# A lone first tile in the batches of a decoder step, its stages interleaved with the next batch's projections, gathers paced closer

## The chip, the cores and the metric

One of the eight cores of a Trainium2 chip runs the kernel. The metric is the device time of one launch in microseconds (us), as the median over several runs; beside it stands one execution that was profiled, from which all rows below come.

## What is computed

One layer of a decoder for a prompt of 1024 tokens (eight tiles of 128) and a sample of 8 x 8 tokens (tile 8, 64 rows), both with the same weights, in float32 with D = 1024:

```
h   = x @ w_in                                # 1024 -> 3072: gate MLP (u, v), retention (q, k, v, g)
mix = concat(spatial_gate(u, v), retention(q, k, v)) @ w_o
x   = layer_norm(ALPHA * x + mix)             # ln1
x   = layer_norm(ALPHA * x + attention(x @ ca_wq, 256 memory tokens) @ ca_wo)   # ln2
q   = x @ peer_wq                             # 8 heads, two halves of 128 keys each
    top 16 of each half -> 256 candidates -> top 16 -> softmax g
act = gelu(u_tab[eidx] . x)                   # 128 experts of 16384 for every token
x   = layer_norm(ALPHA * x + sum(g * act * v_tab[eidx]))                        # ln3
```

The retention carries a state from tile to tile, so the prompt's tiles run in order. The sample attends to its own cached keys and values, 64 blocks of 256 KB.

## The kernel before

Two Python generators emit the whole program. `main` (`front`, then `dense`) and `gathers` each keep an order clock; the one that is behind emits next (the loop at the end of `body`). The clocks are no times: `W.mm` adds 1.3 for every two weight blocks, `front` adds 0.5 when a chunk is done for a tile, a gather adds COST_U (the first 128) or COST_G. The clock becomes the priority from which a list scheduler makes each engine's in-order queue.

**The front** goes through `plan`, a list of (batch, weight, chunk). A weight chunk is 1024 x 512, eight blocks of 256 KB loaded on SP's queue into a ring of NR = 10 (`Weights.load`, line 141). For each chunk all tiles of the batch multiply it (line 149; float32 takes two passes, so 16 passes of 512 columns for a tile and chunk), accumulate in one of three PSUM banks (`mm` twice, `mx` once), and start a generator of small steps (`post_gate`, `post_ret`, `post_res`, `post_att`, `post_att_s` for the sample, `post_peer`) that `step_all` moves on by one step after each quarter chunk. Each batch goes through w_in (6 chunks), w_o, wq, wo (2 each) and pq (4, the expert selection); batch 0 has the memory's wk and wv as well. SPREAD places the pq chunks of one batch between the w_in chunks of the next. Batches before: (0 1), (2 3 8), (4 5), (6 7).

**Experts by gather**, for the tiles in GT = 0, 8, 5, 6, 7: `jobs` lists 576 U gathers and 576 V gathers, one row for each of 128 tokens, 512 KB each, in the order JORD. Each is an indirect DMA that POOL issues (lines 1133, 1136) into one of NG = 6 buffers. A U row set is multiplied and summed on DVE (the dot, line 1068); V rows are combined on PE (line 1096, in pairs). U gathers of a tile need its selection (pq chunk by chunk), V gathers need all of it. The use of a gather is emitted LAG = 3 gathers after its issue.

**Experts by dense matmul**, for the tiles in DT = 1 to 4: after the last pq chunk of such a tile, `post_peer` builds a table G of the gate weights of all 16384 experts: for four tokens at a time one-hot operands (lines 707 to 714, ACT and DVE), four matmuls into the one `gb` bank (line 718), a copy on ACT into the one buffer `big` (line 722), and after 16 tokens a 1 MB store to DRAM (line 726). The flag `gsl` lets one tile build at a time; `gok` (the plan's entry GOK, batch 2's first w_in chunk) lets the first begin. `dense` then streams the whole U and V tables once, 128 blocks: line 977 (h), gelu and the multiplication by G, line 1022 (accumulate), line 1029 (sum on DVE). It reads G back before its first products, and its buffers for V take the place of the table builder's.

`finish` normalises a tile and stores it (line 900). NAT and NA are the numbers of row tiles and of transposed half tiles that the front may hold; `rot` holds the rotary angles of a tile.

Of the kernel before, what the change touches and what calls it, by code (L numbers as in the profile page):

```python
# [22 lines left out]
ALPHA = 2.0 ** 0.25  # L23
EPS = 1e-5
GAM = [1.0 - 2.0 ** (-5.0 - h) for h in range(4)]
BATCHES = [[0, 1], [2, 3, 8], [4, 5], [6, 7]]
TLS = True
MS = ""
SC = 100
# [25 lines left out]
PQT = 2  # L55
PQ = 2
PS = 2
SPREAD = ((0,2,3,5),(0,1,3,4))
PIN = 1
PO = 0  # L60
PG = 0
PC = 0
PP = 0
NR = 10
NAT = 4
NA = 12
NG = 6
LAG = 3
NFL = 4
ND = 2  # L70
GT = [0,8,5,6,7]
DT = [1,2,3,4]
JORD = ("u0","v0","u8","u5 v8","u6 v5","u7 v6","v7")
FB = 2
COST_G = 1.4
COST_U = 1.9
NEG = -3.0e38


def rows(t):  # L80
    return 64 if t == SMP else 128
# [78 lines left out]
def body(ctx: ExitStack, tc: tile.TileContext, a):  # L160
# [14 lines left out]
    def T(shape, tag, bufs=1, dt=F32):  # L175
        return sb.tile(shape, dt, name=tag, tag=tag, bufs=bufs)
# [42 lines left out]

    seq = []  # L220
    plan = []
    for bi in range(len(BATCHES) + 1):
        pq = [(bi - 1, "pq", c) for c in range(4)] if bi else []
        if bi < len(BATCHES):
            names = ("w_in",) * 6 + (() if bi else ("wk",) * 2 + ("wv",) * 2) + ("w_o",) * 2 + ("wq",) * 2 + ("wo",) * 2
            for j, name in enumerate(names):
                plan.append((bi, name, j if j < 6 else j % 2))
                for c in range(4):
                    if pq and SPREAD[bi == 1][c] == j:
                        plan.append(pq[c])  # L230
        else:
            plan += pq
    for _, name, c in plan:
# [23 lines left out]
    st = {}  # L257
# [141 lines left out]
    def aT_tile(t):  # L399
        if t == SMP:  # L400
            x = T([128, 8, 64], "aT", NA)
            return [x[:, 0:4, :], x[:, 4:8, :]]
        return [T([128, 4, 128], "aT", NA), None]

    def aT_half(t, key, j):
        x = st[key, t]
        if x[j] is None:
            x[j] = T([128, 4, 128], "aT", NA)
        return x[j]
# [22 lines left out]
    def post_res(t, c, p, key, res, which):  # L432
        P = rows(t)
        if c == 0:
            if res is None:
                x = T([128, 1024], "nat", NAT)
                nc.sync.dma_start(x[:P], xslice(t))
# [356 lines left out]
    def front():  # L794
        for i, (bi, name, c) in enumerate(plan):
            batch = BATCHES[bi]
            key = KEY[name]
            if (bi, name, c) == GOK:
                st["gok"] = True
            if bi >= XB and name == "pq":  # L800
                st["mxf"] = True
            if plan[i - 1] == (XB - 1, "pq", 3):
                st["mxf"] = True
            if name == "w_in" and c == 0:
                for t in batch:
                    load_split(t, "xT", a["xsT"] if t == SMP else a["xpT"][t])
                    st["rot", t] = T([128, 2, 128], "rot", 3)
                    nc.scalar.dma_start(st["rot", t], a["rot"][t].rearrange("p (a b) -> p a b", a=2))
                if bi == 0:
                    load_small()  # L810
            if name == "w_in":
                gl = T([128, 2, 256], "gl", 2)
                for j, n in enumerate("gb"):
                    w = WORD[c]
                    if w < 2:
                        nc.sync.dma_start(gl[:, j, :], bc(a["gate_ln_" + n][w * 256:(w + 1) * 256], 256))
                    else:
                        nc.sync.dma_start(gl[:, j, :128], bc(a["ret_gn_" + n][(w - 2) * 128:(w - 1) * 128], 128))
            if name == "pq" and c == 0:
                while fin[0] + NFL < sum(1 for b in BATCHES[:bi + 1] for x in b if x in GT):  # L820
                    yield None
            if name == "pq":
                sub = TQ([128, 4, 128], "sub", 1)
                nc.sync.dma_start(sub, a["subT"][:, 4 * c:4 * c + 4, :])
            if name == "w_o" and c == 0:
                load_ln(1)
            if name == "wo" and c == 0:
                load_ln(2)
            tiles = batch
            if name in ("wk", "wv"):  # L830
                tiles = [0, 1]
                if name == "wk" and c == 0:
                    for t in tiles:
                        load_split(t, "memT", a["memT"][t])
            if name == "wq" and c == 0:
                drain("m")
                load_mem(0)
            ps = {}
            for grp in range(KB // GK):
                for t in tiles:  # L840
                    P = 128 if key == "memT" else rows(t)
                    if grp == 0:
                        if c == 0 and key not in ("xT", "memT"):
                            if name == "w_o":
                                drain(t)
                                add(t, post_cat(t))
                            drain(t)
                        if name == "w_in" and c == 0:
                            st["cat", t] = T([128, 1024], "nat", NAT)
                        ps[t] = MM(bi)  # L850
                    p = ps[t]
                    lt = t == tiles[-1]
                    yield from W.mm(i, grp, p[:P], lhs(key, t), lt)
                    if grp < KB // GK - 1:
                        step_all()
                        continue
                    del ps[t]
                    if c == NCH[name] - 1 and name != "wk":
                        del st[key, t]
                    if name == "w_in":  # L860
                        w = WORD[c]
                        add(t, post_gate(t, w, p, gl) if w < 2 else post_ret(t, w - 2, p, gl))
                    elif name == "w_o":
                        add(t, post_res(t, c, p, "x1", None, 1))
                    elif name == "wq":
                        if c == 1 and t == tiles[0]:
                            for x in tiles:
                                drain(x)
                            load_mem(1)
                        add(t, post_att_s(c, p) if t == SMP else post_att(t, c, p))  # L870
                    elif name == "wo":
                        add(t, post_res(t, c, p, "x2", "x1", 2))
                    elif key == "memT":
                        add("m", post_mem(name, c, t, p))
                    else:
                        add(t, post_peer(t, c, p, sub), True)
                    del p
                    yield 0.5
        while any(not e[2] for e in active):
            step_all()  # L880
            yield 3.0

    fin = [0]
    phase = [0]
    jobs = []
    for grp in JORD:
        parts = [[(x[0], int(x[1]), k) for k in range(rows(int(x[1])))] if x[0] == "u" else
                 [(x[0], int(x[1]), c * 32 + r) for r in range(32) for c in range(rows(int(x[1])) // 32)] for x in grp.split()]
        n = max(len(p) for p in parts)
        for i in range(n):  # L890
            for p in parts:
                jobs += p[i * len(p) // n:(i + 1) * len(p) // n]
# [155 lines left out]
    def gathers():  # L1048
# [70 lines left out]
        for m in range(len(jobs) + LAG):  # L1119
            if m < len(jobs):  # L1120
                kind, t, i = jobs[m]
                P = rows(t)
                need = ("v", t) if kind == "v" else ("u", t, 3 if t == SMP else i // 32)
                while need not in done:
                    yield None
                if kind == "u" and i == 0:
                    x2s[t] = TG([128, 1024], "x2g", 1)
                    for j in range(0, 128, P):
                        nc.sync.dma_start(x2s[t][j:j + P], done["x2", t])
                g = TG([128, 1024], "gbuf", NG)  # L1130
                bufs[m] = g
                if kind == "u":
                    nc.gpsimd.indirect_dma_start(out=g, out_offset=None, in_=a["U"],  # L1133
                                                 in_offset=bass.IndirectOffsetOnAxis(ap=done["ix", t][:, i:i + 1], axis=0))
                else:
                    nc.gpsimd.indirect_dma_start(out=g, out_offset=None, in_=a["V"],  # L1136
                                                 in_offset=bass.IndirectOffsetOnAxis(ap=done["ixT", t][:, i:i + 1], axis=0))
            if m >= LAG:
                use(m - LAG)
            yield COST_U if m < 128 else COST_G  # L1140

    clocks = {"f": 0.0, "g": 0.0}
    gens = {"f": main(), "g": gathers()}
    while gens:
        n = min(gens, key=lambda s: clocks[s])
# [71 lines left out]
```

## Time and profile before

| | us |
|---|---|
| median of 3 runs | 3804.4 (3796.0 to 3805.68) |
| the profiled execution | 3794.4 |
| its span, first to last instruction | 3792.6 |
| PE busy | 3375.7 (89%) |
| DVE busy | 2395.5 (63%) |
| ACT busy | 1160.0 (31%) |
| POOL busy | 1546.8 (41%) |
| DMA | 1039.7 MB, 274 GB/s in the mean |

Busy time is the union of an engine's instructions; PE stands for TensorE's matmuls, DVE for VectorE, ACT for ScalarE, POOL for GpSimd, SP for the engine that issues most plain DMAs. PEclk is the granted TensorE clock as a share of 2.4 GHz; a stretch at 1.2 GHz counts as 0.5. A wait is put down to what came last. The execution has a front (the projections end at 1928) and a dense stage (full from 2040 on); the gathers run beside both.

### The profile page before, as it was taken

How to read it: one execution, taken by the hardware profiler on the slowest of the kernel's cores; microseconds unless marked ns; L12 is line 12 of the kernel's file. 1: busy time of each engine (PE TensorE's matmuls, PEld its weight loads, DVE VectorE, ACT ScalarE, POOL GpSimd, SP SyncE). 2: the span in 40 equal slices, each digit the busy share in tenths (PEclk: the TensorE clock that was granted, in tenths of full speed). 3: DMA queues.
4: the chain of work that ended last, by engine and by line, in shares of the span. 5: the costliest groups of instructions: out<-in, count | busy, mean ns of one | idle time of the engine just before them, and what ended most of it. 6: DMA issues, size and time to landing. Idle time of an engine off the chain costs nothing.

```text
span 3792.6 us, 42587 instructions
## 1 busy us (share of the span) xinstructions
PE 3375.7 (89%) x13881; PEld 2028.0 (53%) x13881; DVE 2395.5 (63%) x6366; ACT 1160.0 (31%) x2256; POOL 1546.8 (41%) x1363
## 2 busy tenths in 40 slices
PE   7988875886999989878866999999999999999993
PEld 3444332343443455445445777777667777767650
DVE  2212677715685537996698887777677777777432
ACT  1121212112453464555454222222223222223211
POOL 0000254614254434554433445454444554444443
PEclk9999886887999999988988999999999999999995
DMA  5544475666888789887866989998888989998976
GB/s 192 198 128 152 136 238 211 217 226 237 284 283 286 263 287 334 292 308 254 312 228 230 328 301 336 336 343 312 315 320 315 334 326 330 319 328 297 326 273 232
DMA packets 407358, 1039.72 MB, mean 274 GB/s; under 512 B 37281, under 2 KB 129633, under 8 KB 403041
## 3 DMA queue, kind: packets, MB, share of 16 engines
q0 software_dynamic: 165888, 604.05, 44.3%
q1 hardware_dynamic: 229392, 420.06, 32.5%
q10 hardware_dynamic: 11856, 12.91, 1.0%
q8 instruction: 109, 1.79, 0.2%
q14 instruction: 113, 0.92, 0.1%
HBM read 985.59 MB, written 51.25 MB: 273 GB/s over the span
## 4 chain that ended last, share of the span: by engine, by line
PE 57%; DVE 14%; DMA 13%; issue 11%; POOL 4%; ACT 2%; POOLq 0%; DVEq 0%; SPq 0%; ACTq 0%
PE mm L149 12%; PE h L977 12%; PE mx L149 7%; PE cb L1096 6%; DMA gbuf<-in_V_dram,ixT 6%; DMA gbuf<-in_U_dram,ix 5%; DVE gbuf L1068 4%; PE oa L1022 4%; PE ob L1022 3%; PE od L1022 3%; PE oc L1022 3%; POOL gbuf L1133 2%; PE gb L718 2%; DVE oi L714 1%; POOL gbuf L1136 1%
## 5 line engine op out<-in xcount | busy, mean ns | idle before, releaser
L1133 POOL DMA_INDIRECT gbuf<-in_U_dram,ix x576 | 684.7, 1189 | 878.8 <-DVE hd L1068 476.1
L1136 POOL DMA_INDIRECT gbuf<-in_V_dram,ixT x576 | 634.4, 1101 | 791.5 <-PE cb L1096 359.6
L1068 DVE CUSTOM_DVE_ANT_0 gbuf<-gbuf,x2g 128x1024 f32<-128x1024 f32 x576 | 711.7, 1247 | 361.2 <-DMA gbuf<-in_U_dram,ix 318.2
L149 PE MATMUL mm<-wr,aT 128*128 128x512 f32 (+1 forms) x1632 | 775.4, 614 | 29.9 <-DMA aT<-in_xpT_dram 14.8
L977 PE MATMUL h<-x,uh 128*128 128x512 f32 x2048 | 657.6, 397 | 22.0 <-ACT ga L981 19.4
L149 PEld LDWEIGHTS mm<-wr,aT 128*128 128x128 f32 (+1 forms) x1632 | 292.6, 190 | 414.0 <-issue 366.0
L977 PEld LDWEIGHTS h<-x,uh 128*128 128x128 f32 x2048 | 383.9, 189 | 163.5 <-issue 58.7
L1096 PE MATMUL cb<-gbuf,Z 128*32 128x512 f32 x2304 | 348.4, 642 | 80.4 <-DMA gbuf<-in_V_dram,ixT 78.5
L149 PE MATMUL mx<-wr,aT 128*128 128x512 f32 (+1 forms) x800 | 391.2, 621 | 25.5 <-ACT ret L333 12.9
L977 PE MATMUL h<-x,ul 128*128 128x512 f32 x1024 | 404.2, 395 | 0.0
L917 ACT ACTIVATE vh<-vr 128x1024 fp32r<-128x1024 f32 x128 | 135.3, 1059 | 502.5 <-PE od L1022 494.0
L149 PEld LDWEIGHTS mx<-wr,aT 128*128 128x128 f32 (+1 forms) x800 | 148.2, 193 | 216.5 <-issue 182.9
L714 DVE TENSOR_SCALAR oi<-cst,kt 128x128 f32<-128x128 f32 x512 | 173.5, 385 | 118.6 <-PE gb L718 117.6
L718 PE MATMUL gb<-oi,oj 128*128 128x128 f32 x1024 | 168.0, 310 | 68.3 <-ACT big L722 34.1
L977 PEld LDWEIGHTS h<-x,ul 128*128 128x128 f32 x1024 | 193.1, 189 | 58.5 <-issue 17.6
L718 PEld LDWEIGHTS gb<-oi,oj 128*128 128x128 f32 x1024 | 149.8, 216 | 130.4 <-ACT big L722 54.2
L917 ACT ACTIVATE ah<-ga 128x512 fp32r<-128x512 f32 x128 | 80.7, 631 | 440.5 <-DVE ga L984 388.1
L917 ACT ACTIVATE uh<-ur 128x1024 fp32r<-128x1024 f32 x128 | 135.5, 1059 | 254.9 <-PE h L977 250.7
L722 ACT ACTIVATE big<-gb 128x512 f32<-128x512 f32 x128 | 133.9, 1046 | 223.0 <-PE gb L718 203.6
L918 DVE TENSOR_TENSOR ul<-ur,uh 128x1024 fp32r<-128x1024 f32 x128 | 157.3, 1229 | 59.2 <-ACT uh L917 59.2
L1096 PEld LDWEIGHTS cb<-gbuf,Z 128*32 128x32 f32 x2304 | 50.9, 110 | 227.3 <-issue 118.0
L707 ACT ACTIVATE oj<-cst,kt 128x128 f32<-128x128 f32 x512 | 159.0, 386 | 29.2 <-PE sm L550 17.6
(237 smaller groups left out, 4994.7 us busy)
## 6 DMA issues: line engine op xcount, KB each, us to landing
vr<-in_V_dram SPq DMA_DIRECT2D x128, 512.0 KB, 6.3
ur<-in_Ud_dram SPq DMA_DIRECT2D x128, 512.0 KB, 6.9
wr<-in_w_in_dram SPq DMA_DIRECT2D x192, 256.0 KB, 4.3
wr<-in_pq_dram SPq DMA_DIRECT2D x128, 256.0 KB, 6.2
gsc<-big SPq DMA_DIRECT2D x32, 1024.0 KB, 5.9
G<-gsc SPq DMA_DIRECT2D x32, 1024.0 KB, 16.5
wr<-in_w_o_dram SPq DMA_DIRECT2D x64, 256.0 KB, 4.5
wr<-in_wq_dram SPq DMA_DIRECT2D x64, 256.0 KB, 5.9
```

What stands on the lines that cost most here:

```text
L149: self.nc.tensor.matmul(p, lhsT=lT(k), rhs=w, start=k == 0, stop=k == KB - 1)
L707: nc.scalar.activation(oj[:, r, :], iota, AF.Abs, bias=kt[:, 3, tk + r:tk + r + 1])
L714: x = nc.vector.tensor_scalar(oi, iota, kt[:, 0, tk + r:tk + r + 1], kt[:, 2, tk + r:tk + r + 1], op0=ALU.is_equal, op1=ALU.mult)
L718: x = nc.tensor.matmul(g4[:, r * 128:(r + 1) * 128], lhsT=oj[:, r, :], rhs=oi, start=True, stop=True)
L917: nc.scalar.activation(hi, raw, AF.Copy)
L918: nc.vector.tensor_tensor(lo, raw, hi.bitcast(F32), op=ALU.subtract)
L977: nc.tensor.matmul(p, lhsT=w[:, k, :], rhs=x[:, k, :], start=k == 0 and j == 0, stop=k == 7 and j == 2)
L1022: nc.tensor.matmul(o[j], lhsT=A[i][ia][:, n * 128:(n + 1) * 128], rhs=Vw[i][iv][:, j * 512:(j + 1) * 512], start=b == 0 and ia + iv == 0, ...
L1068: dot = nc.vector.tensor_tensor_reduce(out=g, in0=g, in1=x2s[t], scale=1.0, scalar=0.0, op0=ALU.mult, op1=ALU.add, accum_out=hd[t][:, i:i ...
L1096: nc.tensor.matmul(comb[t][c1 // 2][32 * (q + n):32 * (q + n) + 32, :], lhsT=Z[:, z1 + c1, 31 - r1:63 - r1], rhs=g1[:, n * 512:(n + 1) * 5 ...
L1133: nc.gpsimd.indirect_dma_start(out=g, out_offset=None, in_=a["U"], in_offset=bass.IndirectOffsetOnAxis(ap=done["ix", t][:, i:i + 1], axis=0))
L1136: nc.gpsimd.indirect_dma_start(out=g, out_offset=None, in_=a["V"], in_offset=bass.IndirectOffsetOnAxis(ap=done["ixT", t][:, i:i + 1], axis=0))
```

## The change

The batches become (0), (1 2 8), (3 4 5), (6 7). A hand-written order, HEAD, follows the first batch's w_in, wk and wv: two chunks of the lone tile's w_o, wq, wo or pq, then one ("+") of the next batch's six w_in chunks, and so on. For the later batches the pq chunks stand after w_in chunks 0, 1, 3 and 4. There is one more row tile, one more transposed half tile and one more `rot` buffer. Gathers advance the order clock by COST_F = 1.1 as long as the front runs, where before it was 1.9 for the first 128 and 1.4 after; in the dense stage 1.4 stays. JORD names the gather order anew, and a tile's V gathers can be named in halves (a, b).

```diff
-BATCHES = [[0, 1], [2, 3, 8], [4, 5], [6, 7]]
+BATCHES = [[0], [1, 2, 8], [3, 4, 5], [6, 7]]
-SPREAD = ((0,2,3,5),(0,1,3,4))
+SPREAD = (0,1,3,4)
+HEAD = "w_o w_o + wq wq + wo wo + pq pq + pq pq + +"
-NAT = 4
-NA = 12
+NAT = 5
+NA = 13
-JORD = ("u0","v0","u8","u5 v8","u6 v5","u7 v6","v7")
+JORD = ("u0","v0","u8","v8","u5","v5a","u6 v5b","u7 v6","v7")
-COST_U = 1.9
+COST_F = 1.1
...
-    for bi in range(len(BATCHES) + 1):
-        pq = [(bi - 1, "pq", c) for c in range(4)] if bi else []
+    plan += [(0, n, c) for n, k in (("w_in", 6), ("wk", 2), ("wv", 2)) for c in range(k)]
+    ahead = 0
+    for n in HEAD.split():
+        if n == "+":
+            plan.append((1, "w_in", ahead))
+            ahead += 1
+        else:
+            plan.append((0, n, sum(x[:2] == (0, n) for x in plan)))
+    for bi in range(1, len(BATCHES) + 1):
+        pq = [(bi - 1, "pq", c) for c in range(4)] if bi > 1 else []
         if bi < len(BATCHES):
-            names = ("w_in",) * 6 + (() if bi else ("wk",) * 2 + ("wv",) * 2) + ("w_o",) * 2 + ("wq",) * 2 + ("wo",) * 2
-            for j, name in enumerate(names):
-                plan.append((bi, name, j if j < 6 else j % 2))
-                for c in range(4):
-                    if pq and SPREAD[bi == 1][c] == j:
-                        plan.append(pq[c])
+            for j in range(ahead if bi == 1 else 0, 6):
+                plan.append((bi, "w_in", j))
+                for c, x in enumerate(pq):
+                    if SPREAD[c] == j:
+                        plan.append(x)
+            plan += [(bi, n, c) for n in ("w_o", "wq", "wo") for c in range(2)]
...
-                    st["rot", t] = T([128, 2, 128], "rot", 3)
+                    st["rot", t] = T([128, 2, 128], "rot", 4)
...
+            h = len(part) // 2
+            parts.append({"a": part[:h], "b": part[h:]}.get(x[2:], part))
...
-            yield COST_U if m < 128 else COST_G
+            yield COST_F if phase[0] == 0 else COST_G
```

## Rows read from the trace of the kernel before

**Rows 1.** the page's 40 slices: TensorE's busy tenths

```profile
PE   7988875886999989878866999999999999999993
```

**Rows 2.** windows by stage: length; PE, PEld, DVE, ACT, POOL; clock, DMA share, GB/s

```profile
15.00:182.00 167.00, 157.60 (x440) 75.77 (x440) 40.18 (x164) 29.91 (x70) 8.65 (x16) 0.99 0.58 188
182.00:314.00 132.00, 112.89 (x361) 59.20 (x361) 27.26 (x44) 29.35 (x57) 15.74 (x12) 0.93 0.42 136
314.00:671.00 357.00, 270.26 (x733) 125.70 (x734) 216.84 (x851) 70.46 (x177) 119.04 (x101) 0.80 0.55 183
671.00:951.00 280.00, 227.20 (x825) 105.53 (x825) 132.21 (x265) 59.67 (x133) 116.48 (x80) 0.87 0.67 233
951.00:1242.00 291.00, 284.96 (x1137) 126.97 (x1135) 194.81 (x927) 122.77 (x306) 124.56 (x125) 0.98 0.82 284
1242.00:1424.00 182.00, 166.78 (x750) 86.94 (x750) 86.90 (x315) 99.47 (x232) 69.77 (x68) 0.97 0.79 276
1424.00:1663.00 239.00, 207.32 (x753) 118.50 (x751) 206.54 (x769) 125.54 (x299) 116.80 (x100) 0.91 0.84 304
1663.00:1847.00 184.00, 150.82 (x627) 87.70 (x628) 136.69 (x406) 91.87 (x217) 90.01 (x81) 0.90 0.82 292
1847.00:1928.00 81.00, 81.00 (x304) 40.91 (x302) 64.69 (x266) 35.74 (x86) 32.34 (x30) 0.99 0.80 279
1928.00:2040.00 112.00, 54.29 (x267) 42.40 (x267) 99.01 (x398) 60.96 (x137) 37.01 (x31) 0.73 0.72 244
2040.00:3700.00 1660.00, 1629.30 (x7548) 1154.45 (x7547) 1166.77 (x1921) 422.33 (x535) 780.95 (x686) 0.99 0.89 316
3700.00:3793.00 93.00, 33.09 (x144) 3.78 (x144) 21.52 (x44) 10.69 (x13) 35.22 (x38) 0.53 0.66 229
```

**Rows 3.** windows, line 149 alone: busy us and count of passes

```profile
314.00:671.00 357.00, 207.54 (x417) 78.15 (x418) 0.80 0.55 183
```

**Rows 4.** timeline at the end: start us, us, engine, line, operation, count [idle before]

```profile
3699.65 0.69 DVE L1029 SCALAR_TENSOR_TENSOR acc<-acc,od 128x512 f32<-128x512 f32 x1 [0.20 <-PE od L1022]
...
3765.71 2.38 ACT L1110 ACTIVATE gbuf<-cb 32x512 f32<-32x512 f32 x4 [1.77 <-PE cb L1096]
...
3787.66 1.47 ACTq L900 DMA_DIRECT2D yp_out_dram<-acc  x2
```

**Rows 5.** waits of PE, 314 to 671: us in total, times, longest

```profile
PE sm L318 <- DVE abf L651: 29.0, 1, 29.0
```

**Rows 6.** waits of PE, 1928 to 2040

```profile
PE gb L718 <- ACT big L722: 21.8, 5, 14.1
```

**Rows 7.** windows, line 722 (copy of four tokens of a table)

```profile
888.00:1173.00 285.00, 33.41 (x32) 0.93 0.78 274
1773.00:2020.00 247.00, 33.56 (x32) 0.88 0.76 263
1970.00:2020.00 50.00, 8.50 (x8) 0.80 0.65 222
```

**Rows 8.** windows, line 1096 (combining; four records for one V gather)

```profile
951.00:1242.00 291.00, 53.82 (x320) 8.55 (x320) 0.98 0.82 284
1242.00:1424.00 182.00, 31.25 (x192) 5.16 (x192) 0.97 0.79 276
...
2040.00:3700.00 1660.00, 201.86 (x1496) 29.60 (x1496) 0.99 0.89 316
```

**Rows 9.** windows, line 718 (table matmuls; 256 records a table)

```profile
951.00:1242.00 291.00, 27.41 (x192) 24.69 (x192) 0.98 0.82 284
1242.00:1424.00 182.00, 27.30 (x184) 24.56 (x184) 0.97 0.79 276
```

**Rows 10.** windows, line 1133 (issue of a U gather)

```profile
671.00:951.00 280.00, 82.78 (x59) 0.87 0.67 233
...
2040.00:3700.00 1660.00, 341.93 (x304) 0.99 0.89 316
```

**Rows 11.** timeline of POOL: the first gather

```profile
423.04 1.14 POOL L1133 DMA_INDIRECT gbuf<-in_U_dram,ix  x1 [4.16 <-DVE cd L641]
```

More of the change, by code (lines that the diff above doesn't have):

```diff
@@ L886, in body @@
     for grp in JORD:
-        parts = [[(x[0], int(x[1]), k) for k in range(rows(int(x[1])))] if x[0] == "u" else
-                 [(x[0], int(x[1]), c * 32 + r) for r in range(32) for c in range(rows(int(x[1])) // 32)] for x in grp.split()]
+        parts = []
+        for x in grp.split():
+            t = int(x[1])
+            part = [(x[0], t, k) for k in range(rows(t))] if x[0] == "u" else [
+                (x[0], t, c * 32 + r) for r in range(32) for c in range(rows(t) // 32)]
+            h = len(part) // 2
+            parts.append({"a": part[:h], "b": part[h:]}.get(x[2:], part))
         n = max(len(p) for p in parts)
```

## The prediction

> **What bounds the kernel now.** I read the page first, then one table by stage, then the places where that table shows a loss. The page's slices show where PE has room: sevens and eights in the first half, nines in the second, a drop in the last slice [rows 1]. The stage table is cut where the plan's chunks begin; 16 passes of line 149 are one tile against one weight chunk (I call that a tile-chunk), so the passes between two times tell the place in the plan: 417 between 314 and 671 are 26 tile-chunks [rows 2, 3]. Three things are to be seen.
>
> First, the tail. The last dense accumulation is at 3699.7, but the last output leaves at 3787.7 [rows 4]. In between PE is busy 33 of 93 us, all 144 records being the gathers' combining matmuls [rows 2]: the gathers end last, some 70 us after the dense work.
>
> Second, the dense stage (2040 to 3700) is PE's: 1629 of 1660 us busy, granted clock 0.99 [rows 2]. Less PE work in it, or an earlier start, moves its end one for one.
>
> Third, the front (15 to 2040) holds most idle time: 87 us between 314 and 671 and 53 between 671 and 951, with the clock at 0.80 and 0.87, and 58 of 112 us between 1928 and 2040 [rows 2]. The first of these is not a lack of matmuls: the longest wait there is 29 us of PE for a DVE operation of the expert selection [rows 5], while dots, selection and projections share DVE's one in-order queue. The last is a serial chain: PE waits 22 us for ACT's copies into `big` [rows 6]. That is the building of the one-hot tables G, one tile at a time (`gsl`), one `gb` bank, one `big`. The four tables take 247 to 285 us each (the first and the fourth in [rows 7]; I take 260) though PE's 256 records for one are 37 us of it ((27.4 + 27.3)/376 x 256 [rows 9]), and dense cannot run on before the fourth is done and read back.
>
> **The change part by part.** *Work.* Sixteen chunks times nine tiles plus the memory chunks: 152 tile-chunks and 68 weight chunks before and after; gathers, dots and tables keep their number. Nothing is removed; all is order.
>
> *Lone tile and HEAD.* Batch 0 has 6 + 8 = 14 tile-chunks up to wv. The stage 15 to 182 paid 167/20 = 8.35 us for one [rows 2], so 117 us, to 132. (A single tile per 2.1 MB chunk needs 250 GB/s of weights; that stage moved 188. Bound: nothing, or 6 chunks of 11 us instead of 8.35, +16 us.) HEAD then holds 28 tile-chunks (10 of tile 0, 18 of the next batch's projections). Its worth is cover: the layer norms and attention of tile 0 run beside a three-tile chunk, where before 19 us (182 to 314) stood open. The price lies between 8.35 and that stage's 11.0; I take 9.5, so 266 us, to 398. Moved with the projections are their x loads and 12 gain loads on SP's queue and the rot loads on ACT's; each now stands between tile 0's weight loads and, if its buffer were not free, would hold back the weights behind it. The added buffers (NAT, NA, rot) are there for that: zero with them, one norm chain of 9 to 19 us without.
>
> *Batch 1's second half*, 18 tile-chunks with the sample's attention: 15.6 us each before (671 to 951), now beside denser gathers. I keep 280 us, to 678. Then 27 tile-chunks up to the end of pq chunk 3 of batch 1. The stage 951 to 1242 cost 291 us for 24; without its 54 us of combining [rows 8] and 27 of tables [rows 9] it is 8.75 each, so 236, plus v0 complete (128 gathers at 54/80 = 0.67, 86): 322, to 1000; the last projection chunk to 1026.
>
> *Tables.* Table 1 used to start at 888, because tile 1 was in batch 0. Now tiles 1 and 2 are ready only at about 1015, tiles 3 and 4 together after pq chunk 3 of batch 2. Batch 2's second half is 18 tile-chunks of (182 - 31 - 27)/12 = 10.3, plus a table (37) and v8 (34): 256, to 1282. Then 22 tile-chunks to the end of batch 2's pq: 12.0 each before (264), but DVE was 86% busy there and now gets 12 selections instead of 8, and denser dots [rows 2]; I take 300 (264 to 350), to 1582, and 15 us for the last selection. Tables 1 and 2 (2 x 260 from 1015) are done by 1535, inside that. Table 3 starts at 1600 and takes 260; table 4 runs mostly after the last projection (1582 + 18 + 184 + 81 = 1865), where the copies come 8 in 50 us, 6.25 us each instead of 8 [rows 7]: 200. Reading back took 20 us (2020 to 2040). Dense starts at 1600 + 260 + 200 + 20 = **2080**, 40 us later than now. The front's matmuls end 60 us earlier, but that is not what dense waits for.
>
> *Gathers.* The order clock gives a tile-chunk 4 x 1.3 + 0.5 = 5.7, the front 866 in 1913 us: 2.2 us a unit. A gather at 1.9 or 1.4 is one per 4.2 or 3.1 us (280/59 = 4.7 in 671 to 951 [rows 10]); at 1.1 it is 2.4, just the pace that dense holds: 304 U rows [rows 10] and 1496/4 = 374 V rows [rows 8] in 1660 us, 2.45. So the pace can be met. The first comes after pq chunk 0 of tile 0, at about 340 instead of 423 [rows 11]. From there: u0 and v0 done by 965, u8 and v8 from 1035 (batch 1's selection) to 1350, u5 to 1660, half of v5 to 1820, then u6 with v5: about 660 by 2080, against 1152 - 678 - 36 = 438 by 2040 now. The 490 left need 1200 of dense's 1620 us. **The tail goes**, and what is late next is dense itself. Some 280 V rows are combined before dense instead of 166; dense held 374 of them, now 296, so 78 x 0.54 us (202/374 [rows 8]) = 42 us less PE work.
>
> *The sum,* in the profiled execution: dense's end 3700 + 40 (start) - 42 (combining) = 3698; output of the last tiles 20 us (an estimate: norm, gain, bias and stores took 22 from the last copy at 3765.7 to the last store at 3787.7, for the gathered tile and the dense ones together [rows 4]); 3718 of span, 2 us around it: 3720 against 3794.4. The median of the runs shown lies 0.26% above that execution: **3730 us**.
>
> **A rule weighed.** Between 671 and 951 the core moved 233 GB/s x 280 us = 65 MB [rows 2], 59 x 0.52 = 31 of them gathers; the new pace asks for 103/1.1 = 93 gathers, 49 MB, so 83 MB in 280 us, 296 GB/s. Dense sustained 316 at 0.89 [rows 2]: 263 us, under the stage's time, so the sum above charges nothing. The Trainium skill, "DMA: Bandwidth & Descriptors", section "Issuing engines are not separate DMA queues", says that transfers issued from different engines interleave on the same 16 DMA engines, so that gathers from POOL and weights from SP are rivals. By that rule weights and memory keys come later when gathers are denser; if it bites, it is the third rival.
>
> **The rivals.**
> 1. *Table pair too late (slower).* Two tables after batch 2 instead of one. Each us by which table 3 starts after 1600 is a us of the end. At 1675 the gain is used up; from 1690 on the kernel is slower. It takes stages like 314 to 671 (13.7 us a tile-chunk) where I took 9.5 and 12: 28 x 4.2 = 118 us more. For it: three-tile batches share three accumulator banks, and DVE stalled there before. Against: no dots run during HEAD now. Time 3820 to 3880.
> 2. *The density does not come* (same): gathers wait for buffers (six) and dots, about 450 done by the start of dense, 700 x 2.45 = 1715 us left, and the tail stays. Time 3790 to 3815. Against: dense does hold 2.45.
> 3. *Transfers crowd the front*: weights late by the excess of the stages over 316 GB/s, or DVE at 350 us in batch 3's projections; dense starts at 2120 to 2140. Time 3770 to 3790.
> 4. *Better*: HEAD and batch 1 lose the idle of 87 + 53 us, tables go at the 6.25 us pace; dense starts by 2030. Time 3600 to 3680.
>
> **How the numbers follow.** Forecast (dense starts 2030 to 2120, 3680 to 3770): 0.56. Better 0.16, crowded 0.06, density not reached 0.07, table pair late 0.15. Faster by over 0.3% (what a measurement of this kernel can tell from none): 0.78; within 0.3%: 0.07; slower: 0.15. The range 3625 to 3815 leaves out about 0.06 of the better case below and 0.12 of the late tables above.
>
> **What would show it.** Right: dense sums end last, the last gather is issued hundreds of us before the end, the first before 360, over 600 issued when dense starts; the copies into `big` come in pairs of tables with a pause between, and the last one gates dense with PE idle before it; PE idle in HEAD under 30 us. Wrong: gathers issued until the end, or the front's matmuls ending later than 1928, or table 3 starting well before 1550 or after 1675, or dense not at a clock near 1.00.

## The result and the profile after

The changed kernel takes **3817.1 us** (median of 6 runs, 3814.2 to 3829.2) against 3795.6 for the kernel before in the same series (6 runs, 3791.7 to 3805.7). The ratio is 1.0056 with a 95% interval of 1.0036 to 1.0075: **slower by 0.56%**, where the forecast was 3730 and faster. The profiled execution took 3829.2 us, its span 3827.5.

The stages of the kernel after, as [rows 2] shows them for before: length; PE, PEld, DVE, ACT, POOL; clock, DMA share, GB/s. The cuts are again places in the plan, found by counting the projections' passes: HEAD is 123 to 483 (its last chunk stands alone, 373 to 483), batch 1's second half goes to 773, batch 2's w_in and batch 1's pq to 1134, batch 2's second half to 1373, the rest up to the end of batch 2's last pq chunk to 1633. Table 3 begins at 1750, the projections end at 1993, the first dense accumulation stands at 2186.

```profile
15.00:123.00 108.00, 106.58 (x292) 50.20 (x291) 22.14 (x84) 17.95 (x39) 4.37 (x8) 1.00 0.81 274
123.00:373.00 250.00, 231.10 (x665) 106.26 (x663) 98.80 (x350) 50.44 (x122) 48.43 (x45) 0.93 0.65 219
373.00:483.00 110.00, 49.92 (x143) 26.81 (x142) 88.89 (x293) 19.25 (x47) 68.54 (x51) 0.62 0.70 238
483.00:773.00 290.00, 231.34 (x819) 95.73 (x819) 135.68 (x233) 39.41 (x76) 137.19 (x108) 0.84 0.77 276
773.00:1134.00 361.00, 329.28 (x1249) 138.36 (x1250) 193.54 (x1027) 90.86 (x238) 146.27 (x153) 0.94 0.68 237
1134.00:1373.00 239.00, 207.93 (x854) 116.51 (x853) 160.33 (x359) 116.36 (x256) 131.16 (x114) 0.94 0.84 306
1373.00:1633.00 260.00, 241.06 (x965) 129.14 (x963) 195.56 (x824) 137.28 (x336) 104.65 (x97) 0.95 0.80 283
1633.00:1750.00 117.00, 63.48 (x190) 35.76 (x191) 112.15 (x401) 28.54 (x72) 71.96 (x60) 0.71 0.76 269
1750.00:1993.00 243.00, 207.28 (x854) 114.14 (x857) 181.40 (x579) 116.69 (x279) 134.54 (x113) 0.89 0.83 299
1993.00:2186.00 193.00, 119.33 (x558) 82.51 (x551) 126.67 (x466) 119.56 (x262) 63.19 (x55) 0.67 0.68 248
2186.00:3810.00 1624.00, 1593.61 (x7306) 1155.35 (x7306) 1084.64 (x1736) 420.34 (x530) 632.77 (x555) 0.99 0.81 282
3810.00:3828.00 18.00, 0.00 (x0) 0.00 (x0) 13.00 (x24) 4.86 (x4) 3.04 (x4) 0.57 0.29 117
```

Three rows stand out. In 373 to 483 and in 1633 to 1750 PE is idle for 60 and 54 us and DVE is busy for 89 of 110 and 112 of 117: in the second DVE is the bound, and in the first PE's idle time goes to waits for DVE (32 us) and for ACT (28 us). In 1993 to 2186 PE is idle for 74 us at a clock of 0.67. The dots' share of the first two, DVE on line 1082 alone (each dot leaves two records):

```profile
373.00:483.00 110.00, 47.80 (x77) 0.62 0.70 238
1633.00:1750.00 117.00, 54.65 (x86) 0.71 0.76 269
```

Then the waits of PE: the longest of 373 to 483, the longest of 1633 to 1750, and the sum of 1993 to 2186 (us in total, times, longest):

```profile
PE sm L327 <- DVE g L319: 18.7, 1, 18.7
...
PE gb L701 <- DVE eid L674: 16.5, 1, 16.5
...
PE gb L727 <- ACT big L731: 36.7, 20, 4.2
```

The first two are PE behind DVE: the spatial gate of batch 1, and the transposes that open table 3, for which the last chunk of a selection (`eid`) is missing. The third is the table builder's chain, as [rows 6] had it. The timeline of the table chain's two ends, the start of the dense accumulation, the last gather and the end (start, us, engine, line, operation, count, idle before):

```profile
1749.67 2.08 PE L727 MATMUL gb<-oi,oj 128*128 128x128 f32 x8 [4.88 <-ACT oj L717]
...
2171.32 2.08 PE L727 MATMUL gb<-oi,oj 128*128 128x128 f32 x8 [1.12 <-ACT big L731]
...
2185.83 0.77 PE L1036 MATMUL oa<-vh,ah 128*128 128x512 f32 x1 [9.99 <-ACT ah L931]
...
3538.71 0.95 POOL L1150 DMA_INDIRECT gbuf<-in_V_dram,ixT  x1 [0.30 <-issue]
...
3811.14 0.67 DVE L1043 SCALAR_TENSOR_TENSOR acc<-acc,od 128x512 f32<-128x512 f32 x1
...
3823.70 0.34 ACTq L914 DMA_DIRECT2D yp_out_dram<-acc  x1
```

Against [rows 4] the order at the end is turned round, as forecast: the last gather is issued 272 us before dense ends, and the last store follows the last dense sum by 13 us. The tail (93 us before, 16 now) is gone. But dense starts at 2186 instead of 2062 (the first accumulation of either kernel) and its last sum stands at 3811 instead of 3700. In the two spans: 111.5 us later, 76.7 us of tail saved, **35 us longer**. The first accumulations are not at the same point of PE's work: the kernel before has 179 of the 3072 products `h` behind it at 2062, and at 2040 just as many as the kernel after at 2186 (line 977 before, line 991 after; PE, PEld):

```profile
15.00:2040.00 2025.00, 25.48 (x98) 19.39 (x99) 0.90 0.70 241
...
15.00:2186.00 2171.00, 27.16 (x96) 18.93 (x96) 0.87 0.75 265
```

On equal work dense is thus 146 us later, not 124.

### The profile page after: what moved, and what is told of

Same layout as the page of the kernel before. It is cut to its first block, busy times and chain, and to the rows that moved or that the text cites. A ratio compares the mean times of both kernels' runs of the same rounds, so it can differ in the third digit from the quotient of the medians.

```text
span 3827.5 us, 42619 instructions
## 1 busy us (share of the span) xinstructions
PE 3381.5 (88%) x13881; PEld 2051.3 (54%) x13881; DVE 2414.9 (63%) x6366; ACT 1162.8 (30%) x2254; POOL 1546.3 (40%) x1363
## 4 chain that ended last, share of the span: by engine, by line
PE 56%; DVE 18%; DMA 13%; issue 6%; POOL 4%; ACT 2%; POOLq 0%; SPq 0%; DVEq 0%; ACTq 0%
PE h L991 14%; PE mm L150 11%; DMA gbuf<-in_U_dram,ix 6%; PE cb L1110 6%; PE mx L150 5%; DVE gbuf L1082 5%; DMA gbuf<-in_V_dram,ixT 4%; PE oc L1036 4%; PE oa L1036 4%; PE od L1036 4%; PE ob L1036 4%; POOL gbuf L1147 3%; DVE oi L723 2%; PE gb L727 2%; DMA ret<-in_cv_dram 1%
## 5 line engine op out<-in xcount | busy, mean ns | idle before, releaser
L1147 POOL DMA_INDIRECT gbuf<-in_U_dram,ix x576 | 718.0, 1247 | 661.9 <-DVE hd L1082 342.0
L1150 POOL DMA_INDIRECT gbuf<-in_V_dram,ixT x576 | 607.5, 1055 | 821.6 <-PE cb L1110 481.0
L991 PE MATMUL h<-x,uh 128*128 128x512 f32 x2048 | 648.2, 394 | 1.1 <-ACT gw L683 1.1
L150 PE MATMUL mx<-wr,aT 128*128 128x512 f32 (+1 forms) x800 | 381.9, 610 | 21.6 <-ACT ret L342 19.4
L1110 PE MATMUL cb<-gbuf,Z 128*32 128x512 f32 x2304 | 324.6, 623 | 46.6 <-DMA gbuf<-in_V_dram,ixT 44.0
L727 PE MATMUL gb<-oi,oj 128*128 128x128 f32 x1024 | 190.8, 338 | 123.2 <-DVE oi L723 49.6
L727 PEld LDWEIGHTS gb<-oi,oj 128*128 128x128 f32 x1024 | 166.2, 239 | 185.1 <-ACT big L731 77.2
L150 PEld LDWEIGHTS mx<-wr,aT 128*128 128x128 f32 (+1 forms) x800 | 137.4, 181 | 218.3 <-issue 187.9
L723 DVE TENSOR_SCALAR oi<-cst,kt 128x128 f32<-128x128 f32 x512 | 192.6, 416 | 87.9 <-PE gb L727 78.3
L670 POOL TENSOR_TENSOR cd<-cd,sif 128x512 f32<-128x512 f32 (+1 forms) x72 | 105.4, 1478 | 157.9 <-DVE cd L668 147.8
```

Source lines behind the costliest of these rows:

```text
L150: self.nc.tensor.matmul(p, lhsT=lT(k), rhs=w, start=k == 0, stop=k == KB - 1)
L723: x = nc.vector.tensor_scalar(oi, iota, kt[:, 0, tk + r:tk + r + 1], kt[:, 2, tk + r:tk + r + 1], op0=ALU.is_equal, op1=ALU.mult)
L727: x = nc.tensor.matmul(g4[:, r * 128:(r + 1) * 128], lhsT=oj[:, r, :], rhs=oi, start=True, stop=True)
L991: nc.tensor.matmul(p, lhsT=w[:, k, :], rhs=x[:, k, :], start=k == 0 and j == 0, stop=k == 7 and j == 2)
L1110: nc.tensor.matmul(comb[t][c1 // 2][32 * (q + n):32 * (q + n) + 32, :], lhsT=Z[:, z1 + c1, 31 - r1:63 - r1], rhs=g1[:, n * 512:(n + 1) * 5 ...
```

## The experiments

**Theory P**: the start of dense follows the end of the last table, and that of the last pair of tables waits for batch 2's last selections. **Theory D**: what delays these selections, and batch 1's and 2's projections with them, are the dots, about 1.25 us each on DVE's one in-order queue, that come in greater number when gathers are paced closer. **Rival X**: the denser transfers do it. **Rival B**: the new batches do it, whatever the pace. All landmarks in the table are from the profiles (us); *rows* is the number of gathers issued by the first dense accumulation, and *dense ends* is its last sum on DVE. Each ratio is to the kernel before run in the same series, whose medians were 3799 to 3801 beside the experiments. With the old batches the four tables follow one another from 888 (before, e9) or 989 (e2) on, so table 3 has no such place there; their last one starts at 1784 (before), 1879 (e2) and 1771 (e9). Ahead of the first accumulation stand 96 products `h` in most runs, but 179 in before, 149 in e2, 184 in e8 and 187 in e9; 81 of them take 22 us (2040 to 2062 in before), by which these four runs are further on at that point.

| run | median | ratio to before, 95% | table 3 starts | first acc. | rows | dense ends | last gather |
|---|---|---|---|---|---|---|---|
| before | 3795.6 | 1 | – | 2062 | 443 | 3700 | 3759 |
| after | 3817.1 | 1.0036 to 1.0075 | 1750 | 2186 | 601 | 3811 | 3539 |
| e1_old_pace | 3780.6 | 0.9927 to 0.9966 | 1664 | 2086 | 469 | 3752 | 3734 |
| e2_pace_only | 3805.2 | 1.0003 to 1.0033 | – | 2142 | 515 | 3794 | 3695 |
| e3_hold_u5 | 3785.3 | 0.9949 to 0.9981 | 1716 | 2126 | 515 | 3770 | 3657 |
| e4_thin_u5 | 3745.2 | 0.9829 to 0.9887 | 1696 | 2109 | 601 | 3730 | 3458 |
| e5_no_table4 | 3759.0 | 0.9867 to 0.9921 | 1748 | 2131 | 601 | 3741 | 3469 |
| e6_head_seq | 3773.1 | 0.9902 to 0.9947 | 1686 | 2094 | 505 | 3755 | 3674 |
| e7_v_dense | 3726.7 | 0.9777 to 0.9840 | 1643 | 2041 | 465 | 3699 | 3692 |
| e8_two_banks | **3696.7** | 0.9696 to 0.9760 | 1618 | 2025 | 464 | 3668 | 3661 |
| e9_before_v | 3796.3 | 0.9985 to 1.0006 | – | 2052 | 431 | 3675 | 3757 |
| e10_u_sparse | 3818.1 | 1.0026 to 1.0056 | 1656 | 2020 | 391 | 3659 | 3781 |

**1. The pace alone, both ways.** The kernel after with the old pace, and the kernel before with the new one:

```diff
-            yield COST_F if phase[0] == 0 else COST_G
+            yield 1.9 if m < 128 else COST_G
```

> The changed kernel with the old pace of the gathers (1.9 on the order clock for the first 128, then 1.4); batches, HEAD and gather order as changed. Measured of the changed kernel: table 3's first matmul at 1750, dense's first accumulation at 2186, dense's end at 3810, last gather at 3539, 3817 us. Theory D (the denser dots fill DVE while the last selections of batch 2 are made, so table 3 starts late): table 3 starts by 1680, dense accumulates from 2110 or earlier; about 450 gathers are then issued, 700 x 2.45 = 1715 us are left beside 1620 us of dense, so gathers end last again and the time is 3770 to 3810. Theory P (only the pair of tables behind batch 2 counts): dense still starts at 2150 to 2190 and the time is 3815 or more.

```diff
-            yield COST_U if m < 128 else COST_G
+            yield 1.1 if phase[0] == 0 else COST_G
```

> The kernel before with nothing changed but the gathers' pace, 1.1 on the order clock as long as the front runs: old batches, old plan, old gather order. Theory D: the denser dots crowd DVE beside the selections of batch 0 and batch 2, table 4 is ready after 2040 instead of 2019 and dense accumulates from 2090 to 2140 instead of 2062; but the gathers' tail of 93 us goes, so the time is 3750 to 3800. If the pace alone made the whole loss (denser gathers bring nothing in any order): 3815 or more. If dots beside selections cost nothing: dense from 2065, 3720.

With the old pace table 3 starts 86 us earlier and dense 100 us earlier, and the kernel is faster than before. With the new pace on the old batches dense starts 80 us later, the tail goes all the same, and nothing is won (dense and time 2 and 5 us beyond what Theory D allowed). So the close pace costs 80 to 100 us of dense's start with either batches, and rival B falls as the cause of the loss: the batches with their old pace are 0.54% faster than before. They are not free, though. On equal products `h` their dense starts 46 us after that of before (2086 against 2040), so of the 146 us the pace accounts for 100.

**2. Which part of the gathers costs: transfers or dots.** Tile 5's dots over 64 of the 1024 columns, the gathers unchanged; and tile 5's U gathers held until tile 4 has its last selection chunk:

```diff
-                dot = nc.vector.tensor_tensor_reduce(out=g, in0=g, in1=x2s[t], scale=1.0, scalar=0.0, op0=ALU.mult,
+                w = 64 if t == 5 else 1024
+                dot = nc.vector.tensor_tensor_reduce(out=g[:, :w], in0=g[:, :w], in1=x2s[t][:, :w], scale=1.0, scalar=0.0, op0=ALU.mult,
```

> The changed kernel, but the dots of tile 5 run over 64 of the 1024 columns (this leaves out most of tile 5's dot products); its gathers, their transfers and POOL's issues stay where they are. Theory D (DVE's time is what counts): as with the held gathers, table 3 by about 1660, dense from about 2095, 3730 us. Theory X (the gathers' transfers and POOL's queue delay the selection, not the dots): table 3 stays after 1720 and the time above 3795.

```diff
-                while need not in done:
+                while need not in done or (t == 5 and kind == "u" and ("u", 4, 3) not in done):
```

> The changed kernel, but the U gathers of tile 5 wait (in the order of emission) until the last selection chunk of tile 4 is made, so that their dots no longer lie in DVE's queue beside batch 2's selections. Theory D: table 3 starts at about 1660 instead of 1750, dense accumulates from about 2095 instead of 2186, the gathers still end before dense, and the time is about 3730. Theory P alone: table 3 starts when selection and tables 1, 2 are done as now, dense at 2170 to 2190, 3805 to 3830.

Thin dots alone bring about 72 us, with the same 601 rows moved by the start of dense; the transfers are not what costs, and X falls as the main cause. (The landmarks come later than D's forecast, table 3 at 1696 and dense from 2109, but before X's.) Weights are not late either: in the whole front of the kernel after (15 to 1993) PE waits 2 us for them, most of it here (us in total, times, longest):

```profile
PE mm L150 <- DMA wr<-in_w_in_dram: 1.4, 2, 0.9
```

The stretch of e4 from the end of batch 2's last pq chunk to table 3, whole and then DVE on the dots alone:

```profile
1620.00:1695.00 75.00, 58.43 (x208) 35.83 (x207) 69.47 (x398) 37.67 (x96) 43.78 (x45) 0.82 0.83 294
...
1620.00:1695.00 75.00, 8.90 (x64) 0.82 0.83 294
```

It is 75 us instead of 117, at a higher transfer rate (294 against 269 GB/s). Holding the same gathers was a miss: the dots came in one crowd a little later, 27 us of them still fell into that stretch, and table 3 started at 1716.

**3. The table chain as the gate.** Tile 4's table left out, zeros stored in its place:

```diff
+                if t == 4:
+                    nc.vector.memset(gs, 0.0)
-                for tt in range(0, 16, 4):
+                for tt in range(0, 0 if t == 4 else 16, 4):
```

> The changed kernel without the table of tile 4: its eight stores write a buffer of zeros (this leaves out the 32 groups of one-hot products of that tile). Theory P: table 4 took 157 us (2017 to 2173) between table 3 and dense, so dense accumulates from about 2030 and the time is about 3665. If the front itself were the limit (its last projections end at 1993 and the selections after them at about 2040), dense starts at 2070 to 2100 and the time is 3705 to 3735. If tables were not on the path at all, 3817.

None of the three forecasts came. Dense starts 55 us earlier and the median is 58 us lower; in the profiled executions, of which that of after lies 12 us above its median, dense ends 70 us earlier. So the start of dense is worth about its time. The gain is less than the 157 us that table 4 takes in the kernel after, because the eight stores of zeros still went one by one through `big`, from 2034 to 2118. P also holds across the table: in after, e1, e3 to e7 and e10 the first accumulation follows the last table store by 11 to 14 us. In before, e2, e8 and e9 it follows by 28 to 43 us, as more products `h` are done first.

**4. HEAD without interleaving**, at the old pace, to be read against e1:

```diff
-HEAD = "w_o w_o + wq wq + wo wo + pq pq + pq pq + +"
+HEAD = "w_o w_o wq wq wo wo pq pq pq pq + + + + + +"
```

> As e1_old_pace (new batches, old pace, 3781 us), but HEAD not interleaved: the lone tile's w_o, wq, wo and pq one behind the other, then the six projections of the next batch. If the interleaving is worth what the exposed norms and attention of one tile cost, PE idles 30 to 60 us more before 480, dense accumulates from 2115 to 2145 instead of 2086 and the time is 3805 to 3840; gathers start some 80 us earlier. If it is worth nothing: dense from 2080 to 2095, 3775 to 3785.

The first forecast missed; the second, that interleaving is worth nothing, came within 2 us. HEAD ends 32 us later (496 against 463), although its last chunk takes 65 us instead of 89, but the start of dense is only 7 us later and the time is the same within the intervals. The delay is still there at the end of batch 2's pq (1607 against 1575). It goes behind it: the stretch to table 3 takes 79 us instead of 88, tables 3 and 4 take 395 instead of 411. A late HEAD does not reach dense one for one.

**5. V close, U apart.** V rows are combined on PE and cost DVE almost nothing, so only their pace is raised; then the same pace on the old batches:

```diff
-            yield COST_F if phase[0] == 0 else COST_G
+            yield (1.1 if m < len(jobs) and jobs[m][0] == "v" else 1.9) if phase[0] == 0 else COST_G
```

> The changed kernel with a pace by kind in the front: V gathers at 1.1 (they load PE, not DVE), U gathers at 1.9. Theory D: no dots crowd the selections, so table 3 starts by 1665 and dense accumulates from 2075 to 2090 as in e1_old_pace; V rows come earlier, the gathers end 50 us or more before dense, and the time is 3755 to 3775. If V gathers at 1.1 cost the front as much as dots do (transfers): dense from 2120, 3790 or more.

> The old batches and order with V gathers at 1.1 and U gathers at 1.9 as long as the front runs, so that the worth of the close V pace is seen without the new batches. Theory (close V rows cost little, close U rows cost DVE time, and the batches give little): the first dense accumulation at 2060 to 2090, since the last pair of tables is not delayed by dots, the tail (93 us before) gone or nearly so, 3715 to 3760. Rival (the new batches with their early first gather are what makes the V pace usable): dense starts no later, but gathers still end last by 50 us or more, 3770 to 3800.

On the new batches this is **1.9% faster than before**, better than forecast: dense starts at 2041 instead of 2075 to 2090, though the gathers end only 7 us before it. The stretch up to table 3 has no dot in it any more: tile 5's U rows, begun at 1499 in the kernel after, begin at 1671 here (first all engines, then the dots):

```profile
1559.00:1643.00 84.00, 77.00 (x355) 36.69 (x353) 73.00 (x403) 36.53 (x97) 42.27 (x44) 0.94 0.82 296
...
1559.00:1643.00 84.00, 0.00 (x0) 0.94 0.82 296
```

On the old batches the same pace is worth nothing, so the guess that the pace carries the gain fell: 431 rows by the start of dense, and dense ends 82 us ahead of the last gather:

```profile
3675.21 0.68 DVE L1029 SCALAR_TENSOR_TENSOR acc<-acc,od 128x512 f32<-128x512 f32 x1
...
3756.89 0.95 POOL L1136 DMA_INDIRECT gbuf<-in_V_dram,ixT  x1 [0.39 <-PE cb L1096]
```

There the first gather is at 423, 95 us later than in the new batches, and only 165 V rows are done by the start of dense (192 in e7). So the batches are worth 0.5% with the old pace and 1.9% with this one, and this pace is worth nothing without them. The gather order (JORD) and the buffers came with the batches in all these runs; no run changes them alone.

**6. Two banks for the tables**, on top of e7: batch 3's projections leave the third accumulator bank (`mx`) to tables 3 and 4, which alternate between it and `gb`.

```diff
-XB = 5
-GS = (0,1)
+XB = 3
+GS = (1,2)
```

> As e7_v_dense, but from batch 3 on the projections keep two accumulator banks and every second group of table products takes the third bank (XB = 3, GS = (1,2)). Theory P: tables 3 and 4 are one chain through one bank; with two banks they take 300 to 340 us together instead of 410, dense accumulates from 2000 to 2040, and the time is 3690 to 3730. If the chain is held by the copies and the one store buffer, or if batch 3 loses on two banks what the tables win: dense from 2070 to 2110, 3755 to 3790.

The best of all: tables 3 and 4 take 370 us instead of 385, where 300 to 340 were forecast, and begin 25 us earlier; the time is within the forecast. Table 4 ends 40 us earlier, and dense ends 30 us earlier. PE's waits for ACT's copies between the projections' end and the first accumulation, first e7, then e8; there PE waits 18.6 us for DVE's one-hot operands (`oi`), the next link of the chain:

```profile
PE gb L727 <- ACT big L731: 45.3, 27, 5.2
...
PE mx L727 <- ACT big L731: 3.1, 2, 2.4
```

**7. U still further apart**, on top of e8:

```diff
-            yield (1.1 if m < len(jobs) and jobs[m][0] == "v" else 1.9) if phase[0] == 0 else COST_G
+            yield (1.1 if m < len(jobs) and jobs[m][0] == "v" else 2.6) if phase[0] == 0 else COST_G
```

> The version with two one-hot banks, its U gathers in the front at 2.6 instead of 1.9. Theory D (dots in the front delay the last table pair): with a third fewer dots, table 3 starts at 1580 to 1605 instead of 1622 and the first accumulation comes at 1985 to 2010 instead of 2025; but some 80 to 100 U rows more are left for the dense stage at 2.45 us each, so the gathers end after the dense work again and the time is 3710 to 3780. Rival (what gates table 3 at this pace is the projections, not the dots): table 3 starts within 10 us of 1622, and the time is the tail's alone, 3750 or more.

Both readings missed. Table 3 starts 38 us *later* than in e8. The sample's U rows, all gathered by 1471 in e8, are now spread up to 1749: 19 of their dots lie in the stretch to table 3, where e8 has none (first all engines, then the dots of e10).

```profile
1559.00:1656.00 97.00, 69.71 (x199) 37.07 (x198) 91.52 (x369) 26.86 (x69) 47.97 (x39) 0.82 0.54 185
...
1559.00:1656.00 97.00, 23.35 (x38) 0.82 0.54 185
```

The stretch is 97 us long against 44 in e8, and the dots are 23 us of the difference. So a wider pace of the U rows does not help by itself: it also decides which dots stand ahead of the last selections in DVE's queue. What makes up the other 30 us was not taken apart. And with 391 rows by the start of dense the tail is back: gathers end 122 us after dense.

## Why the prediction failed

The sum was made for the profiled execution: dense from 2080 for 1618 us, then 20. Measured: from 2186, where PE is full, for 1625, then 16. **Of the error of 109 us in the span, 106 are the start of dense.** Followed through the steps, with the same kernel at the old pace (e1) beside it:

| step | predicted | measured | error | e1 |
|---|---|---|---|---|
| end of HEAD | 398 | 483 | +85 | 463 |
| from there to the end of batch 2's pq | 1184 | 1151 | -33 | 1112 |
| from there to table 3's start | 18 | 116 | +98 | 88 |
| table 3's start to table 4's end | 460 | 425 | -35 | 411 |
| from there to dense | 20 | 11 | -9 | 11 |
| start of dense | 2080 | 2186 | +106 | 2086 |

**For DVE the pace was taken as nearly free, and it is not.** At the old pace the forecast start of dense is met within 6 us, but by luck: the steps are wrong by -72 to +70 us and cancel. The close pace adds some 20, 39, 28 and 14 us to the first four steps, 100 in all. The forecast charged the denser dots only within the 36 us added to one stage, and named them again in the third rival. What it booked as gain, 42 us less of dense, came (1625 us, against 1666 in e1 and 1660 before), and was paid with more than twice as much.

**The last selection** is the step that failed most. I set 15 us for it, and nothing had been looked up for that. It is the serial end of the selections on DVE, and it lasts 117 us with 55 us of dots. Thinning most of the dots (e4) leaves 75. With no dot in it, it is 84 us in e7, 87 in e1, but 44 in e8; with 28 us of dots it is 79 in e6 (all engines: e1, e8, e6):

```profile
1576.00:1663.00 87.00, 72.13 (x320) 33.68 (x319) 79.75 (x406) 39.57 (x105) 44.49 (x46) 0.92 0.76 252
...
1574.00:1618.00 44.00, 35.44 (x177) 15.68 (x175) 40.91 (x213) 22.39 (x53) 27.78 (x30) 0.96 0.82 289
...
1607.00:1686.00 79.00, 59.98 (x202) 36.65 (x201) 71.47 (x276) 35.99 (x85) 42.31 (x34) 0.78 0.72 251
```

So of the 98 us some 30 to 55 are the dots, and the rest is the selections and what else stands between them. That the batch of three tiles crowds them is likely but not shown: no run changes that batch alone, and e8 has the same batch and takes 44 us. The warning stood in the rows: in the stage I took for its cost DVE was 86% busy [rows 2], and a full DVE does not give a chunk's end back in 15 us. I charged the crowd on the stage's length (300 for 264), where it did not show (260), and not on its last step, where it did.

**HEAD**, 9.5 us for a tile-chunk, was right for its first 25 of 28 (250 us, 10.0 each), wrong for the last chunk: 110 us for three. The reason that I gave for HEAD's worth, cover for the lone tile's norms, missed what the idle time of 314 to 671 [rows 2] was. 50 of its 87 us lay in the very same chunk, the last w_in of batch 1, after which w_o needs the whole retention and gate; in the trace of before (all engines, then the dots):

```profile
571.00:671.00 100.00, 49.68 (x156) 28.81 (x155) 79.85 (x343) 23.69 (x57) 40.22 (x35) 0.64 0.56 195
...
571.00:671.00 100.00, 24.56 (x41) 0.64 0.56 195
```

DVE is 80% busy there, and the wait of [rows 5] is in it; what waits is the matmul of the spatial gate (line 318). The change moves this chunk 200 us forward and leaves it as it is, with more dots: across the runs with HEAD interleaved it takes 83, 89 and 110 us with 19, 28 and 48 us of dots (e10, e1, after), nearly a us for each us of dots. My argument that no dots run in HEAD was wrong: with tile 0's selection inside HEAD the first gather is at 326, before its end, and the 340 that the prediction gave it lay before the 398 that it gave HEAD's end.

**The rivals.** It was the first, by its condition: table 3 after 1690 makes the kernel slower. It came at 1750; by "each us costs one" that would be 3720 + 150 = 3870 against 3829 measured, the rest being the faster end of the chain. Its condition, HEAD at 13.7 us a tile-chunk, nearly came as a mean (360/28 = 12.9), but the loss lay in one chunk's end and in the last selection, not in slow tile-chunks. Its chance of 0.15 was too low: two serial ends that were not priced, each of about 90 us, were enough. Three signs of being wrong showed: table 3 after 1675 (1750), the front's matmuls ending after 1928 (1993), and PE idle in HEAD for 79 us where under 30 would have been right. Crowding by DVE, a part of the third rival, was the larger cause (thin dots of one tile alone bring dense 77 us earlier in e4), put in the wrong place (batch 3's projections) and priced at half.

**What was right.** The tail goes; the density comes: 601 rows by the start of dense (660 predicted by 2080). Dense, from where PE is full, loses 35 us (42 predicted): 1660 in [rows 2], 1625 now, as 1256 records of combining, 314 V rows, lie in it instead of the 374 of [rows 8] (line 1110 alone, PE and PEld):

```profile
2186.00:3810.00 1624.00, 167.85 (x1256) 24.76 (x1256) 0.99 0.81 282
```

That is 34 us less. Tables go in pairs with a pause between, 1657 to 1750, and table 4 after the projections is quicker than the others (157 us, 200 predicted). But beyond these 34 us the surplus of rows is worth nothing. In every run the gathers left over take 2.31 to 2.46 us each, and dense takes 1610 to 1666 us from its first accumulation to its last sum. Both end together when some 1640/2.4 = 680 are left, that is with about 470 done: 465 in e7, 464 in e8. The change bought 601 of them, over 130 more than could count, and paid for it with the start of dense.

**The rule weighed.** The Trainium skill, "DMA: Bandwidth & Descriptors", section "Issuing engines are not separate DMA queues", says that transfers started by different engines interleave on the same 16 DMA engines. The prediction drew from it that denser gathers would delay the weights. Here the stage 1134 to 1373 moved 306 GB/s in 239 us, 17 us less than predicted, and e4, with every transfer kept, is faster: no run shows that cost as the one that decided.

What stays open: e1 and e7 have the same rows by the start of dense (469 and 465, 277 and 273 of them U) and no dots before table 3, yet e1's dense starts 46 us later. Twenty us of it are table 3's start, 26 the tables 3 and 4 (411 against 385 us); which of the two paces' effects makes the tables slower was not taken apart.

## What to carry to other kernels

Price an order by its serial ends: for each product that a later stage waits for, read the stretch from the last matmul of its input to its first use, on the engine that works there, and add what the change puts into that engine's queue; a stage's mean per unit hides it. Where two streams must end together, work out how much of one must be done when the other starts, and buy no more than that. Pace work by the engine that consumes it: here rows that end on PE could be dense (e7), rows that end on a full DVE could not.

## What the runs showed of the clock

Only a detail was unexpected, and it is small. When the dense accumulation begins in the kernel after, behind 10 us of idle PE, the granted clock is at the lower level (0.50, 1.2 GHz) in 2186 to 2190 and at the higher one (1.00, 2.4 GHz) in 2194 to 2200; in e8, where `h` products keep PE busy up to that point, it is at the higher one from the start. First windows of after (columns as in the stage table), then two of e8:

```profile
2174.00:2186.00 12.00, 1.11 (x3) 0.56 (x4) 6.23 (x11) 3.36 (x5) 2.40 (x2) 0.50 0.76 236
2186.00:2190.00 4.00, 4.00 (x10) 3.13 (x11) 2.49 (x6) 1.45 (x3) 0.22 (x1) 0.50 1.08 371
...
2194.00:2200.00 6.00, 6.00 (x31) 3.97 (x30) 6.00 (x12) 0.00 (x0) 2.70 (x2) 1.00 0.43 116
```

```profile
2010.00:2025.00 15.00, 15.00 (x68) 12.32 (x67) 12.10 (x19) 7.45 (x8) 4.08 (x3) 1.00 0.34 105
2025.00:2030.00 5.00, 5.00 (x23) 4.05 (x22) 5.00 (x8) 1.06 (x1) 4.35 (x3) 1.00 0.73 231
```

Ten passes stand in those 4 us, 31 in the 6 us later: at the later rate ten passes take 2 us, so the low clock costs some 2 us in that window, little beside the 74 us that PE stands idle between 1993 and 2186.
